# A SwiGLU stage on one Trainium2 core: pair 0 also made from seven half products, and other pairs begun ahead

## Chip, core and metric

The kernel runs on one core of a Trainium2 chip. Times are device microseconds (us) of one execution; the kernel before takes 787.64 us, the median of 3 runs (787.57 to 787.65). A matrix product runs on TensorE (PE; its weight loads are PEld), which writes into PSUM banks; VectorE (DVE), ScalarE (ACT) and GpSimd (POOL) do elementwise work; SyncE (SP) and POOL issue most DMA transfers.

## What is computed

One decoder block over 512 tokens of 1024 channels in float32. After two token mixers and their output product, the part that matters here is the channel mixer, with D_FF = 2816:

```python
h = rmsnorm(x, norm2_g[l])
x = x + (jax.nn.silu(h @ ffn_w1[l]) * (h @ ffn_w3[l])) @ ffn_w2[l]
return rmsnorm(x, norm_f_g)
```

## The kernel before

**Exact products from three.** Every float32 operand is split into a high part (a cast on ScalarE to the format that TensorE multiplies in one pass) and a low part (a subtraction on VectorE or POOL). A product is then three matmuls: high x high, high x low, low x high (`mm3`, line 568).

**Pairs.** The 22 column tiles of `ffn_w1` and `ffn_w3` are taken two by two: KF = 11 pairs. Pair 0 is made directly: four banks (two tiles of w1, two of w3), each 8 channel tiles x 3 = 24 matmuls over all 512 tokens, and `ffn_out` (line 1395) takes silu and the product.

Pairs 1 to 10 (`SEVEN`, line 52) are made as a 2 x 2 block product in seven half products instead of eight (Winograd's form of Strassen's scheme). The halves are: tokens LO and HI, channel tiles 0 to 3 and 4 to 7, and the two column tiles of the pair. `f_product` (line 1425) makes one such product for w1 and w3 side by side in one bank: 2 x 4 x 3 = 24 matmuls of 256 tokens. The seven are:

- a11 x b11 into r1 and a12 x b21 into r2 (`Seven.half`); their sum is a quarter of the result, and `Seven.first` adds them on VectorE and takes silu and the product;
- a22 x t4 (`Seven.fourth`, into a bank r4 for the pairs begun ahead; its copy to SBUF on ScalarE is `fourth_end`, line 1499);
- s4 x b22 into r3, s2 x t2 on top of r1, s1 x t1 into r5, s3 x t3 into r7 (`Seven.rest`).

b11 to b22 are quarters of the weights. t1 to t4 are sums of those quarters; they are made early in the kernel, beside the token mixers, in pieces (load, four sums on POOL or VectorE, store to DRAM), four pieces a pair (`f_todo`, line 1107; `make_f_sums`, line 415). The last `F_LATE` pieces are put off: they are placed at position `F_AT` in `out_todo` (line 1290), the list of pieces of the output weight `ffn_w2`, and are made during the feed-forward stage. a11, a12, a22 are parts of the normed input h2. s1 to s4 are sums of its quarters, made by `f_inputs` (line 1410): POOL first adds high and low parts back together (`full`, line 1295), VectorE makes 16 sums of 128x256, ScalarE casts and VectorE subtracts for 8 tiles of 128x512.

**Weights.** All weights pass a list of chunks in order of use (`wchunk`, line 156), mostly 128x1024 float32 (512 KB): loaded by SP into one of 4 raw buffers, cast and subtracted into one of 5 pairs of high and low parts. `weights` (line 202) asks for the chunk that is needed and emits those up to 4 chunks ahead; `lo` names the engine of the subtraction. A narrow pair takes 7 chunks (`f_both`, `f_chunks`), pair 0 took 4.

**Order.** At the end of the mixers' output product TensorE would have nothing to do while the second half of the tokens is normed and turned. There, in an order written out by hand for TensorE, ScalarE and VectorE (line 1539 on), pairs 1 and 2 (`BEGUN`) are begun: `half` needs LO tokens only, and their `fourth` is made as HI tokens arrive (`turn`). Then comes pair 0, then pair 3 is begun (`BEGUN_LATER`: `half`, `first`, `fourth`), then the `rest` of pairs 1, 2, 3, and pairs 4 to 10 whole. From there on the order is program order as the framework's scheduler arranges it.

**Banks.** There are six PSUM banks in one pool (`bank`) and two in another (`bank2`). A begun pair holds the bank of its r1 until the end of its `rest`.

**Output pieces.** `out_step` (line 1379) is called once or more in each pair; by the digits of `OUT_PIECES` it loads the next piece from `out_todo` through POOL's queue, and two steps later stores it; its four sums run on VectorE between these (`due_sums`, line 1371). After the products of a pair, `Sevenfold.pair` (line 1185) makes the inputs of the output product from it; `KEPT` says how many pairs wait for that.

Of the kernel before, what the change touches and what calls it, by code (L numbers as in the profile page):

```python
# [13 lines left out]
P = 128  # L14
# [12 lines left out]
ND = D // P  # L27
# [6 lines left out]
HL = 5  # L34
AHEAD = 4
SUMS_BEHIND = 3
WARM, WARM_LATER = 13, 5

PACK = HB // 2
# [8 lines left out]
PIECES = 4  # L48


OUT_PIECES = {0: "1", 1: "111", 2: "01", 3: "11", 4: "111", 5: "101", 6: "111", 7: "111", 8: "101", 9: "101", 10: "100"}
SEVEN = (1, 2, 3, 4, 5, 6, 7, 8, 9, 10)


BEGUN, BEGUN_LATER = (1, 2), (3,)
SUMS_AT, SUMS_STEP, SUMS_LAG, STORE_LAG = 3, 3, 2, 2
STORED_LAG = 3
SUMS_DENSE, SUMS_OWN, SUMS_EACH = 22, 40, (56, 68)


F_LATE, F_AT, OUT_MIX, MIX_LATE_LAG, LATE_LAG = 2, 6, 1, 2, 8
OUT_IN = 0

KEPT = {2: 1, 3: 2, 4: 3, 5: 4, 6: 5, 7: 6, 8: 7, 9: 7, 10: 7}
# [21 lines left out]
def tile_block(ctx, tc, a, out):  # L86
# [19 lines left out]
    def bank(name):  # L106
        return psum.tile([P, T], F32, tag="mm", name=name)

    def bank2(name):
        return psum2.tile([P, T], F32, tag="cv", name=name)  # L110

    vec, act, pe, pool_e = nc.vector, nc.scalar, nc.tensor, nc.gpsimd
# [43 lines left out]
    def wchunk(key, src, kt, cols, where="hl", lo=pool_e, after=None):  # L156
        chunks.append((key, src, kt, cols, where, lo, after))
# [44 lines left out]
    def weights(key, ahead=AHEAD):  # L202
        i = next(i for i, c in enumerate(chunks) if c[0] == key)
        emit_to(i + 1 + ahead)
        newest["at"] = i
        return held.pop(key)
# [134 lines left out]
    w1 = a["ffn_w1"][0].rearrange("(k p) n -> p k n", p=P)  # L341
    w3 = a["ffn_w3"][0].rearrange("(k p) n -> p k n", p=P)


    KF = NF // 2
    f_sums = {k: dram.tile([P, 2, 2, 1024], F32, tag=f"fs{k}", name=f"fs{k}") for k in SEVEN}

    def f_quarter(n, k, w_, c0, c1):

        c, j = 4 * (int(n[1]) - 1), 2 * k + int(n[2]) - 1  # L350
        return w_[:, c + c0 : c + c1, j * P : (j + 1) * P]
# [7 lines left out]
    def f_both(n, k, lo=vec):  # L359

        def load(raw_t):
            for i, w_ in enumerate((w1, w3)):
                if n[0] == "b":
                    src = f_quarter(n, k, w_, 0, 4)
                else:
                    c, e, _ = WHERE[n]
                    src = f_sums[k][:, i, int(c[1]), :].rearrange("p (k n) -> p k n", k=4)[:, :, e * P : (e + 1) * P]
                newest["any"] = nc.sync.dma_start(raw_t[:, i * T : (i + 1) * T].rearrange("p (k n) -> p k n", k=4), src).ins

        wchunk(f"f{n}_{k}", load, 8, P, lo=lo)  # L370
# [85 lines left out]

    for k in BEGUN:
        for n in ("b11", "b21"):
            f_both(n, k, pool_e if (n, k) == ("b11", 2) else None if k == BEGUN[0] else vec)

    for k in BEGUN:
        f_both("t4", k, vec if k == BEGUN[0] else pool_e)
    for k in range(KF):
        if k in BEGUN + BEGUN_LATER:
            f_both("b22", k)
            f_chunks(k, ("t0",))
            f_both("t3", k)
        elif k in SEVEN:
            f_both("b11", k)
            f_chunks(k)  # L470
        else:
            for j in (2 * k, 2 * k + 1):
                wchunk(f"f1_{j}", w1[:, :, j * P : (j + 1) * P], ND, P, lo=vec if j else pool_e)
                wchunk(f"f3_{j}", w3[:, :, j * P : (j + 1) * P], ND, P, lo=vec)
            if k + 1 in SEVEN:
                for j in BEGUN_LATER:
                    for n in ("b11", "b21", "t4"):
                        f_both(n, j)
    outq = Quartered("o", a["ffn_w2"][0].rearrange("(k p) n -> p k n", p=P), NF // 2, vec, step=2, on_pool=("t4_6",))
    x2_kept = [[dram.tile([P, T], F32, tag=f"x2k{t}{h}", name=f"x2k{t}{h}") for h in range(2)] for t in range(NT)]  # L480

# [86 lines left out]
    def mm3(ps, ws, xs, lo_last=False):  # L568


        n = 3 * len(ws)
        i = 0
        three = [((wh, xh), (wh, xl), (wl, xh)) for (wh, wl), (xh, xl) in zip(ws, xs)]
        if lo_last:
            three = [q[:2] for q in three] + [q[2:] for q in three]
        for l, r in (q for qs in three for q in qs):
            pe.matmul(ps, l, r, start=i == 0, stop=i == n - 1)  # L577
            i += 1

    def w_tiles(key, kt, ahead=AHEAD):  # L580
        h, l = weights(key, ahead)
        return [(h[:, k, :], l[:, k, :]) for k in range(kt)]
# [130 lines left out]
    with tc.manual_schedule(engines={ET.PE, ET.Activation, ET.DVE, ET.SP, ET.Pool}):  # L713
# [31 lines left out]
        r3 = rstd_begin(xt[3][0], junk[0])  # L745
# [4 lines left out]
        r3 = rstd_end(r3, xt[3][1], junk[1])  # L750
# [355 lines left out]

    f_todo = [f_piece(k, i, c) for k in SEVEN for i in range(2) for c in range(2)]
    out_todo = [o_piece(k, c) for k in range(KF) for c in range(2)]
# [258 lines left out]
    o7 = Sevenfold(outq, LATE_LAG)  # L1367
    out_stores, out_n, sums_due = [], [0], []
    out_at, out_steps = [None, None], {k: list(v) for k, v in OUT_PIECES.items()}

# [8 lines left out]
    def out_step(k):  # L1379
        due_sums(True)  # L1380
        stored, begun_ = out_at[1], out_at[0]
        if begun_:
            sums_due.append([SUMS_BEHIND, begun_])
        out_at[1], out_at[0] = begun_, None
        steps = out_steps.get(k)
        if steps and int(steps.pop(0)):
            name, halves, dest = out_todo.pop(0)
            with tc.issue_after(([newest["full"]] * 3 + out_stores)[out_n[0]]):
                out_at[0] = piece_load(name, halves, pool_e), dest
            out_n[0] += 1  # L1390
        if stored:
            with tc.issue_after(newest["full"]):
                out_stores.append(piece_store(*stored, pool_e).ins)

    def ffn_out(j, p1, p3):
        s_ = shortt(f"si{j}")
        act.activation(s_, p1, AF.Silu)

        def make(cs, dst):
            newest["now"] = vec.tensor_tensor(out=dst, in0=s_[:, cs], in1=p3[:, cs], op=ALU.mult).ins  # L1400

        o7.tile(j, make)
# [5 lines left out]
    h2 = parts_of(h2p)  # L1408
# [52 lines left out]
    class Seven:  # L1461
# [36 lines left out]
            self.c21 = longt(f"c21_{self.k}")  # L1498
            act.copy(self.c21, self.r4)

        def rest(self):
            k, got, r1, (u_, v_) = self.k, self.got, self.r1, self.uv
            r3, r5, r7 = bank(f"fr3_{k}"), bank2(f"fr5_{k}"), bank(f"fr7_{k}")
            f_product(k, got, r3, "s4", "b22")
            f_product(k, got, r1, "s2", "t2", True)
            q = shortt(f"q_{k}")
            left_over(act.copy(q, r1).ins)
            f_product(k, got, r5, "s1", "t1")
            add(q, r5, q)
            c12 = shortt(f"c12_{k}")  # L1510
            add(c12, r3, q)
            out_of(c12, u_[:, HI])
            out_step(k)

            o7.release(KEPT.get(k, 0))
            f_product(k, got, r7, "s3", "t3")
            c21 = self.c21
            if c21 is None:
                c21 = shortt(f"c21_{k}")
                act.copy(c21, r7)  # L1520
            else:
                add(c21, r1, c21)
                add(c21, r7, c21)
            add(q, r7, q)
            out_of(q, v_[:, HI])
            if self.c21 is None:
                f_product(k, got, r1, "a22", "t4", True)
                add(c21, r1, c21)
            if k + 1 in SEVEN and k + 1 not in BEGUN + BEGUN_LATER:
                left.append((c21, v_[:, LO]))  # L1530
            else:
                out_of(c21, v_[:, LO])
            out_step(k)
            o7.uv.append((u_, v_))
            o7.waiting.append((k, u_, v_))
# [3 lines left out]
    begun = {k: Seven(k) for k in BEGUN}  # L1539
# [25 lines left out]
    with tc.issue_after(turned[0]), tc.issue_after(turned[1]):  # L1565
# [3 lines left out]
        emit_to(emitted[0] + 3)  # L1569
        f_inputs()  # L1570

    for k in range(KF):
        if k in SEVEN:
            b = begun.pop(k, None)
            if not b:
                b = Seven(k)
                b.half()
                b.first(True)
                out_step(k)
            b.rest()  # L1580
            continue
        o7.release(KEPT.get(k, 0))
        o7.kept = KEPT.get(k, 0)
        for j in (2 * k, 2 * k + 1):
            p1, p3 = bank(f"f1_{j}"), bank(f"f3_{j}")
            mm3(p1, w_tiles(f"f1_{j}", ND), h2)
            mm3(p3, w_tiles(f"f3_{j}", ND), h2)
            ffn_out(j, p1, p3)
        out_step(k)
        if k + 1 in SEVEN:  # L1590
            for j in BEGUN_LATER:
                b = begun[j] = Seven(j)
                b.half()
                b.first()
                out_step(k + 1)
                for c in range(4):
                    b.fourth(c)
                b.fourth_end()


    x2 = [[longt(f"x2b{t}{h}") for h in range(2)] for t in range(NT)]
# [125 lines left out]
```

## Time and profile before

| | us |
|---|---|
| median of 3 runs | 787.64 |
| the profiled execution's own time | 787.45 |
| its span | 785.7 |
| TensorE busy | 777.9 |
| VectorE busy | 682.8 |
| ScalarE busy | 474.6 |
| POOL busy | 362.3 |

All times within a trace count from the start of its span. A row of the chain that ended last gives start, duration, engine, what it writes, the line of the kernel and how many instructions. A row of a timeline gives start, duration, engine, line, operation, output<-inputs (buffer numbers left out), shape, count, and in brackets the idle time of the engine just before it and what ended that. Successive instructions of an engine can overlap a little in the records; matmuls overlap much, so that their spacing, not their duration, counts. In a row by stages there follow for each engine its busy time and number of instructions, then TensorE's granted clock (1.00 is full), the share of the DMA engines' time in use and GB/s.

The tiles of the feed-forward stage are named f (pair 0), fr (products of pairs in seven), hl_fb and hl_ft (parts of chunks of the b and t quarters), hl_f (those of pair 0), hs (s1 to s4), c and q (sums of banks), or (the output product).

### The profile page before, as it was taken

What the parts mean: (1) busy time and instruction counts of PE and PEld (TensorE: products, weight loads), DVE (VectorE), ACT (ScalarE), POOL (GpSimd) and SP (SyncE); (2) the same over time, 40 slices, a digit from 0 to 9 for tenths busy, and PEclk for the clock granted to TensorE, in tenths of its full rate; (3) what the DMA queues carried; (4) which work ended last, traced back from release to release, by engine and by line L of the source; (5) the groups of instructions that cost most, each with busy time, mean ns of one, the idle gap of its engine ahead of it and who ended that gap; (6) DMA issues with size and microseconds to landing.
All of it is one profiled execution on the core that took longest, in us unless ns stands there. A gap on an engine that the chain in (4) does not pass through costs nothing.

```text
span 785.7 us, 12502 instructions
## 1 busy us (share of the span) xinstructions
PE 777.9 (99%) x4327; PEld 680.0 (87%) x4327; DVE 682.8 (87%) x1074; ACT 474.6 (60%) x697; POOL 362.3 (46%) x353
## 2 busy tenths in 40 slices
PE   9999999999999999999999999999999999999996
PEld 8888888888888888888888898999999999888885
DVE  6389998889987988999799869899878888999956
ACT  8543678966785786574235675555554555556844
POOL 4367876789798988654440382122322321000000
PEclk9999999999999999999999999999999999999999
DMA  8556989899899966998978676699998998778652
GB/s 246 164 148 183 290 227 271 239 275 275 249 278 272 274 203 208 331 303 268 306 264 294 189 211 209 192 313 313 348 339 297 325 333 283 226 237 273 196 172 108
DMA packets 188561, 199.04 MB, mean 253 GB/s; under 512 B 15290, under 2 KB 149586, under 8 KB 188498
## 3 DMA queue, kind: packets, MB, share of 16 engines
q1 hardware_dynamic: 178066, 161.80, 68.4%
q0 software_dynamic: 10272, 36.18, 13.2%
q8 instruction: 34, 0.56, 0.3%
q14 instruction: 29, 0.24, 0.1%
q10 hardware_dynamic: 160, 0.27, 0.1%
HBM read 146.30 MB, written 38.80 MB: 236 GB/s over the span
## 4 chain that ended last, share of the span: by engine, by line
PE 98%; DMA 1%; DVE 0%; ACT 0%; SPq 0%; issue 0%
PE z L577 36%; PE fr L1440 25%; PE or L1204 13%; PE yb L577 7%; PE ya L577 6%; PE mxr L1204 5%; PE f L577 3%; PE g L1030 2%; PE fr L1495 1%; DMA x<-in_x_dram 1%; PE tx L638 0%; PE th L622 0%; PE z L695 0%; ACT of L1668 0%; PE orl L1204 0%; DVE n1j L659 0%
## 5 line engine op out<-in xcount | busy, mean ns | idle before, releaser
L830 DVE SCALAR_TENSOR_TENSOR cv<-u,par,cv 128x507 f32<-128x507 f32 (+15 forms) x240 | 162.2, 733 | 4.2 <-ACT cv L826 3.3
L119 POOL TENSOR_TENSOR hl_in<-raw_in,hl_in 128x1024 fp32r<-128x1024 f32 (+1 forms) x52 | 123.8, 2391 | 53.8 <-ACT hl_in L123 44.7
L119 POOL TENSOR_TENSOR fws<-fws 128x256 f32<-128x256 f32 x114 | 92.0, 810 | 44.1 <-DMA fws<-in_ffn_w_dram 38.8
L413 POOL DMA_DIRECT2D ot<-fwso x21 | 15.4, 733 | 132.9 <-DVE fwso L119 125.0
L1440 PE MATMUL fr<-hs_0h,hl_ft 128*128 128x256 f32 x320 | 59.2, 283 | 0.0
L123 ACT CAST hl_ft<-raw_ft 128x1024 fp32r<-128x1024 f32 x40 | 41.7, 1046 | 27.2 <-PE fr L1440 18.5
L119 DVE TENSOR_TENSOR hl_ft<-raw_ft,hl_ft 128x1024 fp32r<-128x1024 f32 x39 | 47.7, 1222 | 10.9 <-ACT hl_ft L123 10.8
L123 ACT CAST hl_in<-raw_in 128x1024 fp32r<-128x1024 f32 x50 | 51.4, 1047 | 1.7 <-PE z L577 1.1
L1440 PEld LDWEIGHTS fr<-hs_0h,hl_ft 128*128 128x128 f32 x320 | 50.6, 192 | 0.0
L1440 PE MATMUL fr<-hs_0l,hl_ft 128*128 128x256 f32 x160 | 45.3, 283 | 0.0
L119 DVE TENSOR_TENSOR hl_fb<-raw_fb,hl_fb 128x1024 fp32r<-128x1024 f32 x29 | 35.5, 1225 | 9.3 <-ACT hl_fb L123 9.3
L123 ACT CAST hl_fb<-raw_fb 128x1024 fp32r<-128x1024 f32 x30 | 31.5, 1049 | 17.9 <-PE fr L1440 8.8
L577 PE MATMUL z<-h10h,hl_in 128*128 128x512 f32 (+1 forms) x108 | 41.1, 382 | 0.0
L577 PE MATMUL z<-h12h,hl_in 128*128 128x512 f32 (+1 forms) x108 | 40.8, 379 | 0.0
L577 PE MATMUL z<-h13h,hl_in 128*128 128x512 f32 (+1 forms) x108 | 40.8, 379 | 0.0
L577 PE MATMUL z<-h14h,hl_in 128*128 128x512 f32 (+1 forms) x108 | 40.8, 379 | 0.0
L577 PE MATMUL z<-h15h,hl_in 128*128 128x512 f32 (+1 forms) x108 | 40.8, 379 | 0.0
L577 PE MATMUL z<-h16h,hl_in 128*128 128x512 f32 (+1 forms) x108 | 40.8, 379 | 0.0
L577 PE MATMUL z<-h11h,hl_in 128*128 128x512 f32 (+1 forms) x108 | 40.8, 379 | 0.0
L577 PE MATMUL z<-h17h,hl_in 128*128 128x512 f32 (+1 forms) x108 | 40.8, 379 | 0.0
L396 POOL DMA_DIRECT2D fwso<-in_ffn_w_dram x42 | 29.9, 716 | 23.7 <-DMA ot<-fwso 21.9
L119 POOL TENSOR_TENSOR hl_ot<-raw_ot,hl_ot 128x1024 fp32r<-128x1024 f32 x1 | 2.4, 2413 | 83.2 <-ACT hl_ot L123 83.2
(949 smaller groups left out, 2629.6 us busy)
## 6 DMA issues: line engine op xcount, KB each, us to landing
raw_in<-in_w_in_dram SPq DMA_DIRECT2D x51, 512.0 KB
fws<-in_ffn_w_dram SPq DMA_DIRECT2D x38, 512.0 KB
raw_ft<-fs SPq DMA_DIRECT2D x34, 512.0 KB
fs<-fws POOLq DMA_DIRECT2D x25, 512.0 KB, 5.2
fwso<-in_ffn_w_dram POOLq DMA_DIRECT2D x42, 256.0 KB, 7.1
ot<-fwso POOLq DMA_DIRECT2D x21, 512.0 KB, 6.0
raw_ob<-in_ffn_w_dram SPq DMA_DIRECT2D x33, 256.0 KB
raw_ot<-ot SPq DMA_DIRECT2D x33, 256.0 KB
```

The source lines that it names most:

```text
L119: return eng.tensor_tensor(out=o, in0=x, in1=y, op=ALU.subtract)
L123: copy(h, full)
L396: queue.dma_start(raw[:, h * n : h * n + n].rearrange("p (e n) -> p e n", n=256), src)
L413: return queue.dma_start(dest, raw.rearrange("p (m n) -> p m n", n=256))
L577: pe.matmul(ps, l, r, start=i == 0, stop=i == n - 1)
L830: vec.scalar_tensor_tensor(out=acc[:, s:], in0=u[c][:, : T - s], scalar=dw(c, s), in1=acc[:, s:], op0=ALU.mult, op1=ALU.add)
L1030: pe.matmul(ps[:HB], head_chunk[0][:ROWS_G, g, h % 2, m, :], ext[h][m][:ROWS_G], start=m == 0, stop=m == 1)
L1204: pe.matmul(banks[i][:, cs], l_[:, ts], r_[:, cs], start=start and n == 0, stop=stop and n == 2, skip_group_check=again)
L1440: pe.matmul(ps[:, HALVES[i]], lw[:, c, :], rx_, start=not (again or i or c or m), stop=bool(i and c == 3 and m == 2), skip_group_check=True,)
L1495: pe.matmul(self.r4[:, HALVES[i]], lw, rx_, start=not (i or c or m), stop=bool(i and c == 3 and m == 2), skip_group_check=True)
```

## The change

Pair 0 is made from seven half products as well. Pairs 0 and 1 are begun ahead, in the written order, in the places of 1 and 2; pairs 2, 3 and 4 are begun later, ahead of the `rest` of pair 0. The chunks are listed in the new order; the first low part after those of the begun pairs, which was pair 0's f1_0 on POOL, is now b11 of pair 2 on VectorE. In the `rest` of pair 0, r7 is in a bank of the second pool. Pair 0 has sums of weights now, so there are 44 pieces of them rather than 40; six rather than two of them are put off, and `OUT_PIECES` has places for 27 pieces rather than 23.

```diff
-OUT_PIECES = {0: "1", 1: "111", 2: "01", 3: "11", 4: "111", 5: "101", 6: "111", 7: "111", 8: "101", 9: "101", 10: "100"}
-SEVEN = (1, 2, 3, 4, 5, 6, 7, 8, 9, 10)
-BEGUN, BEGUN_LATER = (1, 2), (3,)
+OUT_PIECES = {0: "01", 1: "11", 2: "011", 3: "111", 4: "111", 5: "111", 6: "111", 7: "111", 8: "111", 9: "111", 10: "100"}
+SEVEN = (0, 1, 2, 3, 4, 5, 6, 7, 8, 9, 10)
+BEGUN, BEGUN_LATER = (0, 1), (2, 3, 4)
...
-F_LATE, F_AT, OUT_MIX, MIX_LATE_LAG, LATE_LAG = 2, 6, 1, 2, 8
+F_LATE, F_AT, OUT_MIX, MIX_LATE_LAG, LATE_LAG = 6, 6, 1, 2, 8
...
-            f_both(n, k, pool_e if (n, k) == ("b11", 2) else None if k == BEGUN[0] else vec)
+            f_both(n, k, pool_e if (n, k) == ("b11", BEGUN[1]) else None if k == BEGUN[0] else vec)
...
+    for k in BEGUN_LATER:
+        for n in ("b11", "b21", "t4"):
+            f_both(n, k, pool_e if (n, k) in ON_POOL else vec)
     for k in range(KF):
         if k in BEGUN + BEGUN_LATER:
             f_both("b22", k)
             f_chunks(k, ("t0",))
             f_both("t3", k)
-        elif k in SEVEN:
+        else:
             f_both("b11", k)
             f_chunks(k)
-        else:
-            for j in (2 * k, 2 * k + 1):
-                wchunk(f"f1_{j}", w1[:, :, j * P : (j + 1) * P], ND, P, lo=vec if j else pool_e)
-                wchunk(f"f3_{j}", w3[:, :, j * P : (j + 1) * P], ND, P, lo=vec)
-            if k + 1 in SEVEN:
-                for j in BEGUN_LATER:
-                    for n in ("b11", "b21", "t4"):
-                        f_both(n, j)
...
-        def rest(self):
+        def rest(self, last):
-            r3, r5, r7 = bank(f"fr3_{k}"), bank2(f"fr5_{k}"), bank(f"fr7_{k}")
+            r3, r5, r7 = bank(f"fr3_{k}"), bank2(f"fr5_{k}"), last(f"fr7_{k}")
...
+    for k in BEGUN_LATER:
+        b = begun[k] = Seven(k)
+        b.half()
+        b.first()
+        out_step(k)
+        for c in range(4):
+            b.fourth(c)
+        b.fourth_end()
     for k in range(KF):
-        if k in SEVEN:
-            b = begun.pop(k, None)
-            if not b:
-                b = Seven(k)
-                b.half()
-                b.first(True)
-                out_step(k)
-            b.rest()
-            continue
-        o7.release(KEPT.get(k, 0))
-        o7.kept = KEPT.get(k, 0)
-        for j in (2 * k, 2 * k + 1):
-            p1, p3 = bank(f"f1_{j}"), bank(f"f3_{j}")
-            mm3(p1, w_tiles(f"f1_{j}", ND), h2)
-            mm3(p3, w_tiles(f"f3_{j}", ND), h2)
-            ffn_out(j, p1, p3)
-        out_step(k)
-        if k + 1 in SEVEN:
-            for j in BEGUN_LATER:
-                b = begun[j] = Seven(j)
-                b.half()
-                b.first()
-                out_step(k + 1)
-                for c in range(4):
-                    b.fourth(c)
-                b.fourth_end()
+        b = begun.pop(k, None)
+        if not b:
+            b = Seven(k)
+            b.half()
+            b.first(True)
+            out_step(k)
+        b.rest(bank2 if k == 0 else bank)
```

`ON_POOL` is a new, empty tuple.

More of the change, by code (lines that the diff above doesn't have):

```diff
@@ L36 @@
 SUMS_BEHIND = 3
+ON_POOL = ()
 WARM, WARM_LATER = 13, 5
```

## The prediction

> **What bounds the kernel now.** I read the engine totals and the chain of waits first, then what TensorE waited for, then the chain in order of time around the feed-forward stage, and last the other engines stage by stage.
>
> ```profile
> span 785.7 us, 12502 instructions
> PE 777.9 (99%) x4327; PEld 680.0 (87%) x4327; DVE 682.8 (87%) x1074; ACT 474.6 (60%) x697; POOL 362.3 (46%) x353
> PE 98%; DMA 1%; DVE 0%; ACT 0%; SPq 0%; issue 0%
> ```
>
> TensorE is the bound: 98% of the chain that ended last lies on it. The waits of TensorE alone are only two, both in the first microseconds, before the feed-forward stage:
>
> ```profile
> PE warm L546 <- DVE ones L538: 1.1, 1, 1.1
> PE tx L638 <- DVE x L678: 0.6, 1, 0.6
> ```
>
> So in the changed stage TensorE never waits, and its time there is a count of matmuls times their spacing. The chain in order of time (start, duration, what) gives both:
>
> ```profile
> 468.64 21.79 PE f L577 x96
> 490.43 5.75 PE fr L1440 x48
> 496.18 2.88 PE fr L1495 x24
> 499.06 175.68 PE fr L1440 x1464
> 674.74 103.39 PE or L1204 x456
> ```
>
> The first row is pair 0, made directly: 96 matmuls of 512 columns at 21.79 / 96 = 0.227 us. Rows two and three are the two first products and the fourth product of pair 3 (begun later), row four all that is left of pairs 1 to 10: 175.68 / 1464 = 0.120 us for a matmul of 256 columns.
>
> **What the change removes and adds on TensorE.** Away: 96 wide matmuls, 21.79 us. Added: a pair in seven half products takes 7 x 24 = 168 narrow ones, 168 x 0.120 = 20.16 us. The gain with nothing late is **1.63 us**. Seven products for eight sounds like an eighth (2.7 us), but a narrow matmul costs 0.120, more than half of 0.227; that takes back 168 x 0.0065 = 1.1 us. There is no other gain: every other stage of the chain keeps its matmuls. The profiled execution's own time was 787.45 us, 1.75 around its span and 0.19 below the median of 787.64; I take differences from the trace and apply them to the median. Clean, that is 786.0.
>
> The Trainium skill, TensorE: Matmul & The Clock Gate, section Back-to-back issue gap, gives an isolated spacing of N/2.4 + 2.5 ns; an estimate from that page is 96 x 0.2158 - 168 x 0.1092 = 2.4 us of gain, 785.3. The same section puts a sustained stream at about 131 ns for 512 columns, by which (an estimate: 12.6 us for pair 0) splitting into narrow matmuls would lose. The trace's 227 and 120 ns agree with neither, over 96 and 1464 matmuls, so neither gets a chance below.
>
> **What the cover was.** Pair 0 was also a stretch in which the other engines had little to do per microsecond of TensorE: four weight chunks of 128x1024 in 21.79 us, one per 5.4 us. After, pairs 2, 3 and 4 stand there, three chunks in 72 x 0.120 = 8.64 us each, one per 2.88 us, and the stretch from 468.64 until s3 and s4 (the last combined inputs) are needed shrinks from 499.06 - 468.64 = 30.4 us to 3 x 8.64 = 25.9. VectorE makes both the low parts of the chunks and s1 to s4. Its rows in this stage (start, duration) show the real spacing; successive ones overlap by 0.08:
>
> ```profile
> 481.05 0.42 DVE L1153 TENSOR_TENSOR hs<-hf,hf 128x256 f32<-128x256 f32 x1
> 481.38 0.42 DVE L119 TENSOR_TENSOR hs<-hf 128x256 f32<-128x256 f32 x1
> 482.51 1.22 DVE L119 TENSOR_TENSOR hl_ft<-raw_ft,hl_ft 128x1024 fp32r<-128x1024 f32 x1
> 483.65 0.68 DVE L119 TENSOR_TENSOR hs_0l<-hs,hs_0h 128x512 fp32r<-128x512 f32 x1
> 484.25 0.69 DVE L119 TENSOR_TENSOR hs_1l<-hs,hs_1h 128x512 fp32r<-128x512 f32 x1
> ```
>
> A chunk's low part takes 1.14, a 512-wide operation 0.60, a 256-wide one 0.33. Between 468.15 and 494.5 VectorE must do: s1 to s4, 16 x 0.33 + 8 x 0.60 = 10.1; nine chunks (second of pair 2 to b22 of pair 0), 10.3; five `first` steps (an add 0.60, a multiply 0.33), 4.7. Sum **25.1 of 26.4 us**, where the old stretch held:
>
> ```profile
> 468.60:490.40 21.80, 21.80 (x99) 18.04 (x98) 20.97 (x34) 13.93 (x20) 6.97 (x8) 1.00 0.71 219
> 490.40:499.10 8.70, 8.70 (x75) 8.70 (x74) 8.51 (x16) 5.51 (x8) 0.00 (x0) 1.00 0.43 125
> ```
>
> The columns after the length are PE, PEld, DVE, ACT and POOL busy, TensorE's clock, the DMA share and GB/s. VectorE is at 96 to 98% already, but partly with work that was not yet due. Its last low parts there are those of pair 1's t0 and t3, wanted only from 501.9 on (499.06 and one product of 2.88):
>
> ```profile
> 493.48 1.22 DVE L119 TENSOR_TENSOR hl_ft<-raw_ft,hl_ft 128x1024 fp32r<-128x1024 f32 x1
> ...
> 496.81 1.22 DVE L119 TENSOR_TENSOR hl_ft<-raw_ft,hl_ft 128x1024 fp32r<-128x1024 f32 x1
> ...
> 498.55 1.22 DVE L119 TENSOR_TENSOR hl_ft<-raw_ft,hl_ft 128x1024 fp32r<-128x1024 f32 x1
> ```
>
> So it was nearly three chunks ahead at the end. After, it should just keep up, with about none ahead.
>
> Then come five `rest` steps of 96 x 0.120 = 11.5 us (before: three), and from pair 1's second piece on two output pieces in each. Two such stretches of before:
>
> ```profile
> 506.10:517.60 11.50, 11.50 (x98) 11.50 (x97) 10.60 (x20) 5.75 (x8) 2.27 (x4) 1.00 0.83 258
> 517.60:529.10 11.50, 11.50 (x98) 11.50 (x97) 11.27 (x19) 5.72 (x8) 4.43 (x7) 1.00 1.00 331
> ```
>
> VectorE does 10.6 to 11.3 us in 11.5: it bears this, with nearly no reserve, and the second `rest` gets besides it the output inputs of pair 0 (one 512-wide operation, five of 256: 2.3 us) that lay in the old stretch. A full pair and the output stage:
>
> ```profile
> 553.00:573.00 20.00, 20.00 (x169) 20.00 (x168) 17.43 (x29) 10.43 (x16) 6.89 (x10) 1.00 1.01 352
> ...
> 700.00:740.00 40.00, 40.00 (x178) 33.14 (x177) 39.02 (x60) 26.62 (x40) 0.00 (x0) 1.00 0.80 251
> ```
>
> In full pairs there is room (17.43 of 20), so a backlog ends there; and the second row has VectorE at 98% for 40 us with TensorE at work all the time, so a full VectorE alone does not stop it.
>
> **Where small waits are likely.** Four places; each bounded by rows of before.
>
> (1) The chunk emitted ahead of the turn of columns 6 and 7 was f1_0, its low part on POOL; now it is b11 of pair 2 on VectorE, whose order is written out there, ahead of h26l. The rows, each from its engine's timeline:
>
> ```profile
> 460.72 1.05 ACT L123 CAST hl_f<-raw_f 128x1024 fp32r<-128x1024 f32 x1
> ```
>
> ```profile
> 462.37 0.48 DVE L626 SCALAR_TENSOR_TENSOR h26l<-th,par,h26h 128x256 fp32r<-128x256 f32 x1 [1.00 <-ACT h26h L625]
> 469.35 1.60 DVE L119 TENSOR_TENSOR hl_f<-raw_f,hl_f 128x1024 fp32r<-128x1024 f32 x1
> 473.30 3.43 DVE L119 TENSOR_TENSOR hl_f<-raw_f,hl_f 128x1024 fp32r<-128x1024 f32 x2
> ```
>
> ```profile
> 463.65 0.28 PE L1495 MATMUL fr<-h26l,hl_ft 128*128 128x256 f32 x1
> ```
>
> The cast ends at 461.77, a low part takes 1.22 alone and 1.60 beside POOL, so h26l is done at 463.5 to 463.85 and TensorE wants it at 463.65: 0 to 0.2 us late; I take 0.1. (The Trainium skill, SBUF — State Buffer, Who interferes with whom, has an exclusive lock for a VectorE operation with two SBUF inputs beside a GpSimd one; 1.60 against 1.22 agrees.)
>
> (2) t4 of pair 2 is wanted by 468.64 + 50 x 0.120 = 474.64. In its place before stood the first of the two low parts from 473.30, which ends at about 475.0: 0 to 0.4 late, less if the two sums ahead of it come behind; I take 0.2.
>
> (3) PSUM. Five begun pairs hold five of the six banks; r4 of pair 4 has the sixth. r3 of pair 0 comes right behind and needs that bank: ScalarE must first copy r4 out. That copy, for pair 3:
>
> ```profile
> 499.10 0.59 ACT L1499 COPY c<-fr 128x512 f32<-128x512 f32 x1
> ```
>
> TensorE's fourth product ended at 499.06, so a bank is free 0.63 later, some 0.7 with the signal; if a cast of 1.05 stands ahead of the copy, 1.7. No wait if the other product of pair 0 that is ready (s2 with t2, into r1) is put ahead. Nearest row 0.7, half the time: I take 0.35. Behind it on TensorE stands everything.
>
> (4) VectorE's sums as above, 0 to the price of the slow rival. I take 0: it is 5% short of full, and adds can wait for a bank's length.
>
> Costed at nothing: ScalarE, which has room (13.93 of 21.80 busy above), and the weight sums of pair 0, four pieces more. The steps ahead of the feed-forward stage take 40 - 2 = 38 pieces before and 44 - 6 = 38 after, so these stages keep their count. The four come later, on POOL's queue and VectorE:
>
> ```profile
> L413 POOL DMA_DIRECT2D ot<-fwso x21 | 15.4, 733 | 132.9 <-DVE fwso L119 125.0
> L396 POOL DMA_DIRECT2D fwso<-in_ffn_w_dram x42 | 29.9, 716 | 23.7 <-DMA ot<-fwso 21.9
> ```
>
> A piece is two loads and a store, 2.2 us of POOL, which stands 0.00 busy in the row from 490.40; VectorE's 4 x 0.33 per piece is in the sums above. The six late ones are pieces 7 to 12 of 27, read by about pair 5 and wanted by pairs 9 and 10. If POOL had no room, its store would be late, for which the wait of 125.0 us on VectorE says that it is not POOL that is late.
>
> Sum: 1.63 - 0.1 - 0.2 - 0.35 = 0.98 us. **Forecast 786.7 us.**
>
> **Rivals.**
>
> *Clean* (786.0): the order of issue absorbs all three waits. For it: TensorE shows not one wait in the feed-forward stage now, at up to 98% of VectorE. Against: three new tight places, each of which needs only 0.1 us to show. Below 786.06 it is faster by over 0.2%, which is about what a measurement of this kernel can tell from no change.
>
> *VectorE becomes the bound* (slower). From 468.15 to the end of the fifth `rest` TensorE needs 26.4 + 57.6 = 84.0 us. VectorE needs 25.1 + a first `rest` with one piece 9.7 (10.6 to 11.3 less 4 x 0.33) + a second of 11.3 + 2.3 + three of 11.3 = 82.3. It stands idle 4% even in its fullest old stretch (20.97 of 21.80), 3.3 us of 84, and low parts beside POOL cost 0.4 more, some three times: 86.8. If each shortfall reaches TensorE, 2.8 us are lost, and with the bank at 1.7 and (1), (2) at their ends 0.6, 5.1: 787.64 - 1.63 + 5.1 = 791.1; with the bank at 0.7, 790.1. From 1.0 us of shortfall on (beside the 0.65 of places 1 to 3) nothing is gained, from 2.6 on it is slower by over 0.2%. Against: the low parts are asked for up to four chunks ahead, and the output stage's 98% above.
>
> *DMA comes late.* Chunks are 512 KB, a piece 512 KB in and 512 KB out:
>
> ```profile
> raw_ft<-fs SPq DMA_DIRECT2D x34, 512.0 KB
> fs<-fws POOLq DMA_DIRECT2D x25, 512.0 KB, 5.2
> ```
>
> Each `rest` with four chunks and two pieces moves 4.2 MB in 11.5 us, 364 GB/s, where a share of 1.01 (the row from 553.00) moved 352. Four of them fall 46 x 12 / 352 = 1.6 us behind. Then 787.6 or so, if nothing is loaded ahead; but four raw buffers hold 11.5 us, so mostly hidden.
>
> That the change doesn't do what it says is out: the matmuls are counted in the code.
>
> **How the numbers follow.** Forecast (some of the waits, 786.2 to 787.4) 0.43; clean 0.20; VectorE 0.25; DMA or a mixture near no change 0.12. Faster by over 0.2% (under 786.06) is most of clean: 0.17. Slower by over 0.2% (over 789.2) is the VectorE case with part of the mixture: 0.27. Within: 0.56. The range runs from the clean case less 0.1, 785.9, to the VectorE case with the bank at 0.7, 790.1; some 0.15 is left out.
>
> **What would show it.** Right: the chain shows no pair 0 by wide matmuls, 1680 + 168 narrow ones at 0.120, and TensorE waits under a microsecond, at h26l, t4 of pair 2 and r3 of pair 0. Wrong: waits of TensorE on low parts (hl_fb, hl_ft) or on sums hs from 477 to 552 mean the VectorE rival; ScalarE casts waiting for raw chunks mean DMA; a spacing other than 0.120 would break the gain itself.

## The result, and the profile after

The kernel after takes **793.25 us** (median of 4 runs, 793.15 to 794.66) against 787.61 (4 runs, 787.53 to 787.65): ratio 1.0075, 95% interval 1.0063 to 1.0088. It is slower by 5.6 us, 3.15 above the top of the range on record. The profiled execution took 793.16 us, with a span of 791.4 (before 785.7). In the kernel after, helper functions stand one line lower than before and the feed-forward code four lines higher: L1436 is the matmul of `f_product`, L1491 that of `fourth`, L1495 the copy in `fourth_end`, L1474 the copy of r1, L1455 the multiply of `first`, L120 subtracts, L124 casts.

The page of the kernel after, engine totals and the shares of the chain:

```profile
PE 779.7 (99%) x4399; PEld 684.9 (87%) x4399; DVE 691.7 (87%) x1101; ACT 478.6 (60%) x705; POOL 366.9 (46%) x360
PE 96%; DVE 2%; ACT 1%; DMA 1%; issue 0%; SPq 0%; ACTq 0%
```

There are 72 matmuls more (168 - 96), as counted. But 2% of the chain now lies on VectorE and 1% on ScalarE, where before each had 0%; the DMAs keep their 1%. What TensorE waited for in the kernel after (us in total, times, longest):

```profile
PE fr L1436 <- DVE hl_ft L120: 4.4, 1, 4.4
PE warm L542 <- DVE ones L534: 1.1, 1, 1.1
```

One new wait, 4.4 us in one piece, for the low part of a t chunk. The chain of the kernel after, in order of time, around it:

```profile
465.17 1.43 PE fr L1491 x12
...
493.29 1.15 DVE hl_ft L120
494.48 7.87 PE fr L1436 x51
502.35 2.88 PE fr L1491 x24
505.23 175.05 PE fr L1436 x1457
680.28 19.75 PE or L1200 x87
```

The wait ends at 494.48. From 505.23 on 1457 matmuls run without a break at 175.05 / 1457 = 0.120 us, so the many pieces behind it cost nothing here. But the 51 right behind the wait took 7.87 us, 0.154 each, where 51 x 0.120 is 6.12. The same stretch by stages (columns as in the prediction; the last row is a part of the one above it):

```profile
477.30:485.90 8.60, 8.60 (x74) 8.60 (x74) 7.69 (x14) 7.15 (x10) 0.00 (x0) 1.00 0.87 241
485.90:494.50 8.60, 4.25 (x36) 4.00 (x34) 8.60 (x16) 4.82 (x8) 0.00 (x0) 1.00 0.69 216
494.50:506.10 11.60, 11.60 (x82) 11.44 (x83) 5.53 (x9) 4.27 (x8) 0.00 (x0) 0.85 0.31 98
495.10:498.40 3.30, 3.30 (x18) 3.30 (x17) 2.68 (x5) 1.29 (x3) 0.00 (x0) 0.50 0.62 185
```

VectorE is full while TensorE waits (8.60 of 8.60), and behind the wait TensorE's granted clock is 0.85 on average, and 0.50 from 495.1 to 498.4. TensorE's timeline shows what stood at its head:

```profile
489.36 0.38 PE L1436 MATMUL fr<-hs_0h,hl_ft 128*128 128x256 f32 x1
489.58 0.28 PE L1436 MATMUL fr<-hs_0l,hl_ft 128*128 128x256 f32 x1
489.70 0.32 PE L1436 MATMUL fr<-hs_0h,hl_ft 128*128 128x256 f32 x1
489.85 0.28 PE L1436 MATMUL fr<-hs_0l,hl_ft 128*128 128x256 f32 x1
494.48 0.50 PE L1436 MATMUL fr<-hs_0h,hl_ft 128*128 128x256 f32 x2 [4.35 <-DVE hl_ft L120]
```

Those are products with hs, the combined inputs, of **pair 0**: s2 x t2, and a part of s1 x t1, which reads the same tiles. They stand here although pair 4 has had only its second product made: of its 72 begun matmuls, 48 (the first product, and the 24 of L1491 at 502.35) come behind. In the order in which the kernel is built, TensorE's list reads: second product of pair 4, 31 matmuls of pair 0 (s2 x t2 has only 24, so 7 are of s1 x t1), first product of pair 4, fourth product of pair 4. In program order pair 0 comes behind all of pair 4, 48 x 0.120 = 5.8 us later. ScalarE's timeline tells why. Its last cast of the combined inputs, and what follows:

```profile
494.80 0.62 ACT L124 CAST hs_1h<-hs 128x512 fp32r<-128x512 f32 x1 [0.85 <-DVE hs L120]
495.32 1.07 ACT L1495 COPY c<-fr 128x512 f32<-128x512 f32 x2
```

The two copies at 495.32 are those of r4 of pairs 2 and 3, whose fourth products TensorE left at 477.83 and 486.47 (the next product's first matmul starts there). So the two banks were held for some 17 and 9 us more. With r1 of pairs 0 to 3 that makes six: no bank was free for r1 of pair 4, and the framework's scheduler put ahead on TensorE what needs no bank of this pool: s2 x t2 on top of r1 of pair 0, and some of s1 x t1, whose r5 is in the second pool. Their operands come at the end of VectorE's list for this stretch.

The difference of the two profiled executions, by rows: -1.63 for the matmuls; +0.33 near the start of the kernel, where the stream that stood at 23.37 in before stands at 23.70; +0.2 at the turn of columns 6 and 7; +0.2 at t4 of pair 2; +4.5 for the wait with the signal; +1.75 for the low clock. The sum is 5.35; the output product's first row is 680.28 - 674.74 = 5.54 later.

### The profile page after: what moved, and what is told of

Read it like the earlier page. It is cut to its first block, busy times and chain, and to the rows that moved or that the text cites. A ratio compares the mean times of both kernels' runs of the same rounds, so it can differ in the third digit from the quotient of the medians.

```text
span 791.4 us, 12738 instructions
## 1 busy us (share of the span) xinstructions
PE 779.7 (99%) x4399; PEld 684.9 (87%) x4399; DVE 691.7 (87%) x1101; ACT 478.6 (60%) x705; POOL 366.9 (46%) x360
## 4 chain that ended last, share of the span: by engine, by line
PE 96%; DVE 2%; ACT 1%; DMA 1%; issue 0%; SPq 0%; ACTq 0%
PE z L573 36%; PE fr L1436 25%; PE or L1200 13%; PE yb L573 7%; PE ya L573 5%; PE mxr L1200 5%; PE g L1026 2%; PE fr L1491 1%; PE warm L542 1%; DMA raw_fb<-in_ffn_w_dram 1%; PE tx L634 0%; PE th L618 0%; PE z L691 0%; DVE hl_ft L120 0%; DVE hs L120 0%
## 5 line engine op out<-in xcount | busy, mean ns | idle before, releaser
L120 POOL TENSOR_TENSOR hl_in<-raw_in,hl_in 128x1024 fp32r<-128x1024 f32 (+1 forms) x52 | 123.3, 2381 | 54.1 <-ACT hl_in L124 46.4
L120 POOL TENSOR_TENSOR fws<-fws 128x256 f32<-128x256 f32 x114 | 92.6, 815 | 42.8 <-DMA fws<-in_ffn_w_dram 37.5
L1436 PE MATMUL fr<-hs_0h,hl_ft 128*128 128x256 f32 x352 | 66.9, 288 | 4.4 <-DVE hl_ft L120 4.4
L124 ACT CAST hl_ft<-raw_ft 128x1024 fp32r<-128x1024 f32 x44 | 45.9, 1048 | 27.1 <-DMA raw_ft<-fs 20.2
L1436 PEld LDWEIGHTS fr<-hs_0h,hl_ft 128*128 128x128 f32 x352 | 56.9, 196 | 4.6 <-DVE hl_ft L120 4.6
L124 ACT CAST hl_fb<-raw_fb 128x1024 fp32r<-128x1024 f32 x33 | 34.5, 1048 | 41.1 <-DMA raw_fb<-in_ffn_w_dram 33.8
L120 DVE TENSOR_TENSOR hl_ft<-raw_ft,hl_ft 128x1024 fp32r<-128x1024 f32 x43 | 52.6, 1223 | 2.8 <-ACT hl_ft L124 2.7
L124 ACT CAST hl_in<-raw_in 128x1024 fp32r<-128x1024 f32 x50 | 51.5, 1047 | 2.1 <-DMA raw_in<-in_w_in_dram 2.1
L1436 PE MATMUL fr<-hs_0l,hl_ft 128*128 128x256 f32 x176 | 50.4, 287 | 0.0
L120 DVE TENSOR_TENSOR hl_fb<-raw_fb,hl_fb 128x1024 fp32r<-128x1024 f32 x32 | 39.0, 1225 | 9.9 <-ACT hl_fb L124 9.9
L120 POOL TENSOR_TENSOR hl_ot<-raw_ot,hl_ot 128x1024 fp32r<-128x1024 f32 x1 | 2.4, 2406 | 82.1 <-ACT hl_ot L124 82.1
```

Of the source, the lines that this page charges most:

```text
L120: return eng.tensor_tensor(out=o, in0=x, in1=y, op=ALU.subtract)
L124: copy(h, full)
L1436: pe.matmul(ps[:, HALVES[i]], lw[:, c, :], rx_, start=not (again or i or c or m), stop=bool(i and c == 3 and m == 2), skip_group_check=True,)
```

## The experiments

**Theory: order of slots.** Tiles with the same tag share a fixed number of places in SBUF, the slots, and the framework hands them out in program order. The destinations of the copies (`c21`, tag "long") come behind the combined inputs of `f_inputs` in it, so that the copies wait for those though slots are free. That holds two banks, reorders TensorE, and makes the wait. **Rival A: VectorE** has more to do than the stretch holds (98 to 100% busy), and would be late in any order. **Rival B: DMA**: the chunks land late (ScalarE's waits for raw b and t chunks sum to 33.8 + 20.2 us in after, against 3.2 in before). Ratios are to the kernel before, run on the same chip. From e3 on all are made on e1's kernel.

**e1_c21_early.** The three destinations get their slots ahead of `f_inputs`, each by a write of one column on POOL:

```diff
+        for j in (2, 3, 4):
+            kept[j] = longt(f"c21_{j}")
+            pool_e.memset(kept[j][:, :1], 0.0)
         f_inputs()
...
-            self.c21 = longt(f"c21_{self.k}")
+            self.c21 = kept.pop(self.k, None) or longt(f"c21_{self.k}")
```

> The changed kernel, with one byte-wide write (a memset of one column on POOL) to each of the tiles c21 of pairs 2, 3 and 4 ahead of f_inputs, so that their slots are handed out before those of s1 to s4; nothing else differs. In the built order the copies of r4 on ScalarE then no longer stand behind f_inputs, pair 4's r1 gets a bank, and TensorE's order is begun 2, 3, 4 and then pair 0's rest. Theory (slot order): the 4.4 us wait for a low part of t0 and the low clock behind it (7.87 us for 51 matmuls rather than 6.12) go; TensorE wants pair 0's rest at about 495.4 and s1 to s4 end at about 497, so 0 to 2 us of wait are left: 786.6 to 788.8. Rival A (VectorE has too much work, whatever the order): the wait only moves, 791 to 793. Rival B (chunk loads by DMA come late): TensorE stops at a chunk's low part in the begun pairs, 790 to 793.

Measured: 787.36 (10 runs, 786.63 to 790.37), before 787.59; ratio 1.0005 (0.9994 to 1.0017). The profiled execution took 786.66. TensorE's waits in it, both at the start of the kernel:

```profile
PE warm L542 <- DVE ones L534: 1.1, 1, 1.1
PE tx L634 <- DVE x L674: 1.0, 1, 1.0
```

Its chain in the feed-forward stage, all on TensorE but 0.02 us:

```profile
463.90 0.71 PE fr L1493 x6
...
468.84 5.76 PE fr L1436 x48
474.60 3.07 PE fr L1493 x24
477.67 5.76 PE fr L1436 x48
483.43 2.88 PE fr L1493 x24
486.31 5.76 PE fr L1436 x48
492.07 2.88 PE fr L1493 x24
494.95 0.72 PE fr L1436 x6
495.66 0.02 issue
495.68 178.09 PE fr L1436 x1482
673.77 103.39 PE or L1200 x456
```

Pairs 2, 3 and 4 are whole, 48 and 24 each, and only then pair 0 starts. The copies of r4 (L1497 in this kernel) stand where they belong, on ScalarE's timeline:

```profile
480.60 0.58 ACT L1497 COPY c<-fr 128x512 f32<-128x512 f32 x1
...
487.81 0.58 ACT L1497 COPY c<-fr 128x512 f32<-128x512 f32 x1
...
495.04 0.59 ACT L1497 COPY c<-fr 128x512 f32<-128x512 f32 x1 [0.37 <-PE fr L1493]
```

VectorE in the same windows as above:

```profile
477.30:485.90 8.60, 8.60 (x74) 8.60 (x73) 7.87 (x14) 7.36 (x11) 0.00 (x0) 1.00 0.90 245
485.90:494.50 8.60, 8.60 (x74) 8.60 (x73) 8.60 (x16) 6.34 (x10) 0.00 (x0) 1.00 0.52 159
```

It is just as full, 8.60 of 8.60, and TensorE does not wait, since it asks in the order in which VectorE delivers. The theory holds: the order of slots costs 5.9 us of median (793.25 against 787.36). As causes of the 4.4 us, A and B fall: neither VectorE's work nor the transfers were cut.

One thing is left: ten runs of e1 lie between 786.63 and 790.37, while 25 runs of before beside them lie within 0.94 us. Six lie at 787.54 or below, four from 788.57 up.

**e2_parts.** After's kernel with `f_inputs` cut in four, one part ahead of pair 2 and one behind `fourth_end` of each of pairs 2, 3 and 4, so that program order itself gives the slots in time (VectorE's and ScalarE's order changes with it):

```diff
-        f_inputs()
+        f_inputs([0])
...
         b.fourth_end()
+        f_inputs([BEGUN_LATER.index(k) + 1])
```

> The changed kernel with f_inputs cut in four: the sums for one channel tile ahead of pair 2, the next three behind the fourth product of pairs 2, 3 and 4. Slots are then asked for in another order: c21 of pair 2 stands behind two parts of eight tiles rather than eight. Theory (slot order): r4 is copied in time, TensorE's order is 2, 3, 4; but the last sums are traced later and may come later: 786.5 to 789.5. Rival A (VectorE's work): 791 to 793. Rival B (DMA): 790 to 793.

Measured: 789.38 (10 runs, 788.24 to 791.98), ratio 1.0027 (1.0016 to 1.0038). The wait of 4.4 us is gone in this way too. TensorE's largest waits in its profiled execution, apart from the one in the first microseconds:

```profile
...
PE fr L1436 <- ACT c L1495: 0.5, 1, 0.5
PE tx L634 <- DVE x L674: 0.5, 1, 0.5
PE fr L1491 <- DVE hl_ft L120: 0.5, 1, 0.5
PE fr L1436 <- DVE hl_fb L120: 0.4, 1, 0.4
```

The row on ScalarE (ACT c, the copy of r4) is the bank that the prediction saw: r3 of pair 0 waits for the copy of r4 of pair 4, 0.5 us. It shows here because a cast of 1.03 us runs on ScalarE ahead of that copy, the case that the prediction bounded by 1.7; 14 matmuls of pair 0, put ahead on TensorE, hide the rest.

**e3_early_pool.** b11 of pair 2 has its low part on POOL, as pair 0's chunk had in that place before (`ON_POOL = (("b11", 2),)`).

> As the first, and the low part of b11 of pair 2 on POOL again, where pair 0's first chunk had its own. Theory: h26l is no longer behind a low part on VectorE, so the 0.2 us of TensorE's wait at the turn of columns go, and VectorE has 1.14 us less in a full stretch: 0.2 to 1.2 us below the first run. Rival A (VectorE's work decides): 1.1 us or more below the first. Rival B (DMA): equal to the first, within 0.3 us.

Measured: 788.11 (10 runs, 787.31 to 789.85), ratio 1.0010 (1.0001 to 1.0020): not the gain expected. The 0.2 at h26l is gone, but low parts of t chunks are 0.5 late at 475 and 0.3 at 496. The profiled execution was this kernel's slowest, 789.85, so it shows where time goes in a high run: those two waits, 0.5 for x2b and 0.3 for hl_ob (tiles of the output product), 1.4 at the start. Its chain runs back from there through transfers, where e1's has none behind 463 us. Each row goes from the issue to the landing:

```profile
498.78 5.64 DMA raw_ft<-fs
...
506.85 8.84 DMA raw_ft<-fs
```

**e4_half_loads.** Half of each output piece's load is left out, with the DMA time that goes with it.

```diff
+        if name[0] == "o" and queue is pool_e:
+            pool_e.memset(raw[:, n:], 0.0)
+            halves = halves[:1]
```

> Kernel e1 (slots of c21 first), whose ten runs went from 786.63 to 790.37, with half of each output piece's load left out in the feed-forward stage: one transfer of 256 KB rather than two, the other half set to zero on POOL, so the sums of the output weight are not those of the reference; VectorE's work and all stores are the same. 21 x 0.26 = 5.5 MB less, some 27 GB/s in 200 us, where the DMA share was 1.01 to 1.05. Theory (the spread of e1 is DMA at its limit in pairs 3 to 10: chunks land late, and small waits appear in this and the output stage): the runs close up, 786.3 to 787.2, ACT's waits for raw chunks fall below 15 us (31.8 in e1's profile). Rival (VectorE, 17 to 19 us of 20 in these stages, is late by itself): median and spread as e1, 787.4.

Measured: 786.96 (10 runs, 786.66 to 788.01), ratio 0.9992 (0.9983 to 1.0002). The runs lie within 1.35 us rather than 3.74, and ScalarE waits for raw b and t chunks 12.8 us in place of the 34.8 of e1's profile (17.5 for t, 17.3 for b; the 31.8 of the expectation is not their sum). ScalarE's waits in e4:

```profile
ACT hl_ft L124 <- DMA raw_ft<-fs: 6.9, 7, 1.7
ACT hl_fb L124 <- DMA raw_fb<-in_ffn_w_dram: 5.9, 5, 2.2
```

With less to move, the spread is smaller: none of ten runs lies above 788.01, while of the twenty of e1 and e10 (below) seven lie at 788.57 or higher. Were there no difference, that would still come up about once in 26 times. This kernel computes less, so it is no version.

**e5_pool_sums.** The four sums of each output piece and late piece on POOL in place of VectorE, in the feed-forward stage.

> Kernel e1 with the sums of the late pieces on POOL rather than VectorE (27 pieces x 4 operations x 0.33 = 36 us less on VectorE, nothing less on DMA). Theory (DMA): median and spread as e1 or worse, 787 to 790, since the chunks still land late. Rival (VectorE): the runs close up at 786.2 to 786.8.

Measured: 808.93 (4 runs, 805.14 to 812.94), ratio 1.0269 (1.0226 to 1.0312). It was meant to lighten VectorE and loaded it. Its low parts of b chunks took 1.589 us each against 1.225 in e1, those of t chunks 1.462 against 1.222. The groups of e5 by line, then its row by stages, then TensorE's longest wait:

```profile
L120 DVE TENSOR_TENSOR hl_ft<-raw_ft,hl_ft 128x1024 fp32r<-128x1024 f32 x43 | 62.9, 1462 | 14.8 <-ACT hl_ft L124 14.5
L120 DVE TENSOR_TENSOR hl_fb<-raw_fb,hl_fb 128x1024 fp32r<-128x1024 f32 x32 | 50.6, 1589 | 9.1 <-ACT hl_fb L124 9.0
```

```profile
486.00:512.00 26.00, 13.15 (x81) 12.54 (x80) 26.00 (x24) 11.01 (x16) 24.02 (x27) 0.75 0.79 248
```

```profile
PE fr L1436 <- DVE hl_ft L120: 8.6, 1, 8.6
```

Beside a POOL that is 92% busy VectorE is full for 26 us and TensorE waits 8.6 in one piece (and 3.8 in another, for a b chunk). So VectorE has no reserve in that stretch: e1 passes, and operations that are longer by 20 to 30% do not. For the spread it tells nothing.

**e6_late2 and e8_late4.** Two and four pieces put off in place of six, and four and two places less for pieces in the feed-forward stage:

```diff
-F_LATE, F_AT, OUT_MIX, MIX_LATE_LAG, LATE_LAG = 6, 6, 1, 2, 8
+F_LATE, F_AT, OUT_MIX, MIX_LATE_LAG, LATE_LAG = 2, 6, 1, 2, 8
```

(e8: 4, and the places of pairs 6 and 9 "101"; e6: pairs 5, 6, 8 and 9 as well.)

> Kernel e1 with only two weight sums put off, as before the change (42 of 44 made beside the token mixers), and four places fewer in the output pieces of pairs 5 to 9 (one each in 5, 6, 8 and 9). Both 4.2 MB of DMA and 5.4 us of VectorE leave the full stage. Either theory: the spread becomes smaller, median 786.2 to 787.0, unless the four sums hold something up beside the mixers. If it stays at 787.4 and up, neither is the cause.

> Kernel e1 with four weight sums put off rather than six, and two places fewer among the output pieces (pairs 6 and 9): 2.1 MB and 2.7 us of VectorE less in the full stage, two pieces more beside the token mixers, where four more cost 6 us in e6 since they ran into the mix stage. Theory: if two still fit, 786.4 to 787.0 with a spread under 1.5 us; if not, some 2 to 4 us more, all of it before 445 us, and the feed-forward stage without waits.

Measured: e6 793.98 (4 runs, 793.83 to 794.16), ratio 1.0080 (1.0063 to 1.0097); e8 789.52 (7 runs, 789.12 to 790.87), ratio 1.0029 (1.0018 to 1.0040). Neither waits in the feed-forward stage. TensorE's longest wait in e6:

```profile
PE mxr L1200 <- ACT mxus3h L124: 2.8, 1, 2.8
```

The loss lies ahead, in the mixers' output product (mxr), into which the pieces that are not put off now run: 2.8 us in e6, 2.5 in e8 over four waits. In e6 the low clock comes on top, 0.50 from 425.0 to 431.7, around the end of that wait. The 84 matmuls that follow the mixers' product on the chain start at 456.62, in e1 at 449.65: the whole loss is made by then. To put off six is part of what makes the change possible.

**e7_one_sum.** Three of the four sums of each piece in the feed-forward stage are left out, and nothing takes their place.

> Kernel e1 with one of the four sums of each late piece made on VectorE and three left out (the weight sums are not those of the reference); all transfers stay. 27 x 3 x 0.33 = 27 us less on VectorE, nothing less on DMA: the counterpart of e4. Theory (the spread of e1 is DMA at its limit): median and spread like e1's in the same call, ACT's waits for raw chunks as there, some 30 us. Rival (VectorE is late): the runs close up, 786.2 to 786.9.

Measured: 798.36 (4 runs, 793.97 to 800.48), ratio 1.0130 (1.0098 to 1.0162). Missed by far: VectorE has room, and TensorE waits more. ScalarE's longest waits in e7, and a full pair by stages:

```profile
ACT hl_fb L124 <- DMA raw_fb<-in_ffn_w_dram: 65.4, 23, 8.8
```

```profile
552.00:572.00 20.00, 17.63 (x134) 17.43 (x134) 15.26 (x23) 10.21 (x16) 5.28 (x7) 0.91 0.92 308
```

VectorE is at 15.26 of 20.00 us, ScalarE waits for b chunks up to 8.8 us at once, and TensorE stands, up to 2.4 us in one piece. So it is not the sums on VectorE that make chunks late behind 500 us. Why they land still later here is not shown; that pieces are done sooner, and their transfers so stand beside other ones, is only argued.

**e9_late4_pool.** e8 with b11 of pair 2 on POOL.

> Kernel e8 with the low part of b11 of pair 2 on POOL. Theory: the 0.2 us at h26l go, nothing else changes: 0.0 to 0.4 us below e8. Rival (e3 was slower than e1 because this holds POOL up): 0.3 us or more above e8.

Measured: 789.15 (10 runs, 787.63 to 791.79), ratio 1.0019 (1.0009 to 1.0029). It lies between e8 and e3, 0.4 below e8 as the theory had it, and has waits of both kinds: on sums in the mixers' product, on low parts of t chunks in the feed-forward stage.

**e10_again.** e1's kernel on another chip.

> Kernel e1 once more, on the chip of these runs, as their base. Theory (DMA): a spread of 2 us or more again, from 786.5 up; median 787 to 788. Rival (the spread was that chip's): a spread under 0.5 us.

Measured: 787.03 (10 runs, 786.61 to 791.71), before 787.54 (22 runs, 787.35 to 788.15); ratio 1.0004 (0.9990 to 1.0018). Seven runs at 787.18 or below, three from 788.99 up: the spread is the kernel's and not one chip's.

**e11_one_moved and e12_two_moved.** One and two places for pieces moved from the full pairs to where the DMA engines had room:

```diff
-OUT_PIECES = {0: "01", 1: "11", 2: "011", 3: "111", 4: "111", 5: "111", 6: "111", 7: "111", 8: "111", 9: "111", 10: "100"}
+OUT_PIECES = {0: "11", 1: "11", 2: "011", 3: "111", 4: "111", 5: "111", 6: "111", 7: "101", 8: "111", 9: "111", 10: "100"}
```

(e12: pair 2 "111" and pairs 6 and 8 "101", pair 7 "111".)

> The kernel of e1_c21_early, with one place for a piece moved from pair 7 to the rest of pair 0, where the DMA engines were in use for 0.85 of the time (495 to 506) rather than 1.01 to 1.05. If the spread between single runs of e1_c21_early (3.7 us) comes from chunks that land late in the full pairs, one piece less there takes a good part of it: median 786.7 to 787.0, runs within 2.5 us, ratio 0.999. If VectorE, with 10.75 of 11.0 us busy in that rest, is what decides, its four sums more make TensorE wait there by 0.3 to 1.3 us: 787.7 to 788.6. If neither, 787.2 with the same spread.

> The kernel of e1_c21_early, with two places for pieces moved from pairs 6 and 8: one to the rest of pair 0, one to the step in which pair 2 is begun (468 to 477, DMA engines in use for about 0.75 of the time). By the DMA theory the spread falls further than with one: median 786.6 to 786.9, runs within 2 us, ratio 0.9988. If VectorE decides, its eight sums more (2.6 us) between 470 and 506, where it has 24.84 of 26.4 and 10.75 of 11.0 us busy, make TensorE wait 0.5 to 2.6 us for low parts or for s3 and s4: 788 to 790. If neither, 787.2 with the same spread.

Measured: e11 787.72 (12 runs, 786.63 to 791.09), before 787.41 (23 runs, 787.06 to 788.81); ratio 1.0005 (0.9995 to 1.0014). e12 788.98 (11 runs, 787.26 to 790.52), ratio 1.0017 (1.0008 to 1.0025). Nothing is gained: in e11 the spread did not close (4.5 us). Its median stands at the edge of what VectorE would cost, but its profiled run of 787.68 has no TensorE wait in the feed-forward stage. The chain of e11 at the start of pair 2:

```profile
469.84 5.76 PE fr L1436 x48
```

In e1 it is 468.84: that run's 1.0 us over e1's profiled one lies ahead of pair 2, most of it at the start of the kernel (TensorE's first stretch of 48 matmuls starts at 17.07 in e1 and at 17.80 here, which is 0.7 of it). In e12 the median is higher, as VectorE's eight sums more between 470 and 506 would have it; but the trace, of a run at 787.95, shows only one wait of 0.2 in the stage, for an addition on VectorE. So the place of that loss isn't shown.

## Why the prediction was wrong, point by point

**The step that failed** is place (3), the sentence "Five begun pairs hold five of the six banks; r4 of pair 4 has the sixth." It counted banks by when their contents end. The r4 of pairs 2 and 3 still held two, because a copy on ScalarE also needs a place to write to, and that place came behind the combined inputs in the order of slots. I had bounded the wait at r3 of pair 0 by 0.7 us, or 1.7 behind a cast. What came was no wait there: one of 4.5 us on an earlier matmul, with 1.75 us of low clock behind it, 6.2 us in all. e1 and e2 show it by two different cures. None of the rivals had this mechanism; that the VectorE rival at its far end, 791.1, comes nearest is chance.

The same place had an escape: no wait "if the other product of pair 0 that is ready (s2 with t2, into r1) is put ahead". That product is the one that was put ahead, and it was not ready. The move that I counted as a help is the loss. It was also in sight that its operands end VectorE's list, for the sum of 25.1 of 26.4 us was made up to s3 and s4, and the two low parts of t0 that this product reads are not even in it: to ask for s2 x t2 some 5.8 us early asks more than that sum can give.

**The gain of 1.63 us** was right. In e1, where nothing else is in the way, the output product starts at 673.77 against 674.74, 0.97 us sooner, where the forecast's sum was 0.98. The terms there: 0.21 at place (1), by the row at 463.90 against before's at 463.69; 0.19 at place (2), 3.07 in place of 2.88 for the fourth product of pair 2; some 0.28 at place (3), where 6 matmuls of pair 0 go ahead, r3 then starts 0.18 late and 0.10 more is lost at its second matmul. I had 0.1, 0.2 and 0.35. e2 has 0.5 at (3), inside its bounds. The profiled time of e1 is 786.66 and the forecast 786.7: it was a forecast of this kernel at its best, not of the one that was built. That run is the second fastest of e1's ten, whose median is 787.36; the forecast had nothing for the spread.

**The rival VectorE** was not the cause, but near: with VectorE full, e1 passes without a wait and e5 shows what a somewhat slower VectorE does. The sign that the prediction gave for it (waits on hl_ft between 477 and 552) did appear, at 494, and would have named the wrong cause. The wait's releaser is VectorE; the reason is the order on TensorE. Only the list of instructions told them apart.

**The rival DMA** was priced at 1.6 us and "mostly hidden". In the profiled run of after it is hidden: 1457 matmuls at 0.120 follow. But in e1 the runs lie up to 3.7 and 5.1 us apart (e1, e10). e4, which moves less, has a smaller spread, and the trace of e3's slowest run has transfers of up to 9.95 us in its chain; e11 and e12, which moved the same load elsewhere, did not close it. That late transfers have a part in it is likely by this, but not shown; which of them, and why in some runs only, stays open.

**The cover of pair 0.** That its 21.8 us were the slack of the other engines was right as a description, and e1 shows that VectorE can do without it.

No version that computes everything beat the kernel before: e1 and e10 are the best, with intervals that hold 1.

## What to carry to other kernels

A bank is free when the copy out of it has run, and the copy runs when its destination has a slot: follow that one step further before you count banks, above all where a tile with a long life shares a tag with many that are listed ahead of it. Where a change adds work in front of a hand-ordered or scheduled stretch, compare the built order of each engine's instructions with program order; a product put ahead of its turn can wait longer than the thing it was to hide. And an engine at 98 to 100% need not cost anything while it is asked in the order in which it delivers: here VectorE at 8.60 of 8.60 us cost 4.5 us in one order and nothing in the other.

## What the runs showed of the hardware that was not expected

Behind a wait of 4.5 us TensorE was slower. Its timeline in the kernel after, 1 us behind the wait:

```profile
495.30 0.41 PE L1436 MATMUL fr<-hs_0l,hl_ft 128*128 128x256 f32 x1
495.51 0.63 PE L1436 MATMUL fr<-hs_0h,hl_ft 128*128 128x256 f32 x2
495.94 0.41 PE L1436 MATMUL fr<-hs_0l,hl_ft 128*128 128x256 f32 x1
```

Three matmuls start in 0.64 us, 0.21 each in place of 0.120; by 498.5 the spacing is back. The granted clock in between is 0.50, as the row from 495.10 above shows. The same stands at the long waits of other runs: a clock of 0.50 from 556.0 to 559.3 in e7, behind a wait of 2.4 us; from 425.0 to 431.7 in e6, with a wait of 2.8; from 505.9 to 516.0 in e5, where TensorE waits 8.6 us until 510.7. The waits of 0.5 us in e2 and e3 in the feed-forward stage brought nothing like it. So in these runs each wait of TensorE from 2.4 us up cost more than it lasted: here 1.75 us on 4.5. In the middle of these kernels the longest wait without a lower clock is 0.8 us (e7); where between 0.8 and 2.4 us it begins is not shown.
